# DeltaNet: the blocks M for the row-by-row inverse come by four transfers of 32 partitions instead of one of 128, and are first touched one step later

## The chip, the cores and the metric

One core of a Trainium2 chip. The metric is the device time of one execution in microseconds (us); lower is better.

## What is computed

One decoder layer of 1024 tokens with d_model 1024: a combined projection, dilated attention (A), gated DeltaNet (B), a mix of both, a hierarchical mixture of experts and a per-layer embedding. The change lies in B. It has 8 heads of width 128 and works in chunks of 64 tokens; each chunk needs the inverse of a unit lower triangular matrix:

```python
a_mat = jnp.where(tril_strict, jnp.einsum('nbhid,nbhjd->nbhij', kbeta, kc) * decay_mat, 0.0)
eye = jnp.eye(CHUNK, dtype=jnp.float32)
t_mat = lax.linalg.triangular_solve(eye + a_mat, jnp.broadcast_to(eye, a_mat.shape),
                                    left_side=True, lower=True, unit_diagonal=True)
u = jnp.einsum('nbhij,nbhjd->nbhid', t_mat, vc * bc[..., None])
w = jnp.einsum('nbhij,nbhjd->nbhid', t_mat, kbeta * jnp.exp(gcum)[..., None])
...
def step(state, xs):
    qd, ui, wi, ai, gl, kt = xs
    v_new = ui - jnp.einsum('bhcd,bhde->bhce', wi, state)
    o = jnp.einsum('bhcd,bhde->bhce', qd, state) + jnp.einsum('bhij,bhje->bhie', ai, v_new)
    state = state * jnp.exp(gl)[..., None, None] + jnp.einsum('bhcd,bhce->bhde', kt, v_new)
    return state, o
```

## The kernel before

The layer is one program. In its DeltaNet stage (about 650 to 1290 us of the span) two things run interleaved. The first is the projection: `channels` is a generator that multiplies the normed tokens with the weights of one job (128 output channels) after the other, in two halves of 512 tokens; each half sums 24 matmuls of 128x512 (L37 to L39, three for each product, since both factors are split into a high and a low part) into the PSUM tile mm, of which there are two buffers. Every `next` of it issues six of these matmuls. The last one of a half calls `done`: for q, k and v that is `conv` (L627 to L638, on ScalarE and VectorE), for z it is `job_z` (L669 on ScalarE, then L671 on VectorE; L671 is what sets the PSUM buffer free). Weight tiles wraw come by SP's DMA queue, are split on ScalarE (whi, L182) and VectorE (wlo, L183).

The second is the head's own work. `delta_net` counts steps, 32 for each head; the table P says at which of a head's steps which function issues its instructions: decay at 4 and 5, kk (which fills nat, the blocks of a_mat) at 10 and 13, `solve` at 15, `turned` at 37, `after` at 43. A function with `yield` goes on at the next step. After a step's functions the projection gets its six matmuls. The Python order is only the start: a scheduler in the compiler of the program then fixes the order of the instructions on each engine, and each engine runs its own in that order.

`solve` inverts the 32x32 blocks on the diagonal, 8 token tiles x 4 blocks in one head. L751 writes them from nat to a DRAM tile dA of 32 rows of 1024 numbers, one row for each block. L753 reads that back as M: each of the 4 groups of 32 partitions gets all of dA, 512 KB in all, and each group then computes 8 of the 32 columns of every block's inverse (tu). After three yields L757 sets M's diagonal to one, and 31 row steps follow on VectorE, a multiplication (L764) and a sum (L766) each, whose size grows from row to row, with a yield after every fourth. Then L770 writes tu to DRAM (dT), L774 reads it back as um, `turned` transposes blocks of um (L781), and `after` extends the inverse to 64x64 and runs the scan over chunks: PE multiplies the state S with k (pks, L911), VectorE makes vb of it (L913), PE multiplies vb with um (pvn, L917), ScalarE copies it (vn, L920), PE makes the state's increment (pds, L930) and VectorE the next S (L933 for the first chunk, L936 for the others). So the scan of one head and `solve` of the next share VectorE.

M has one buffer, as most tiles of pool dn. D, the decays, is also filled by a broadcast of 512 KB, in `rows` (L711): one row of 1024 numbers to 128 partitions. L802 multiplies D with PE's products of q and k (pkq, L800); L806 prepares the norms of q (sq); L700 those of k (sk), which the head's later work starts from; L681 transposes k, q and v on PE.

Of the kernel before, what the change touches and what calls it, by code (L numbers as in the profile page):

```python
# [610 lines left out]
class Head:  # L611
# [131 lines left out]
    def solve(self):  # L743


        k, nc, dn = self.k, self.k.nc, self.k.dn
        dA = k.dram.tile([32, 1024], F32, name="dA", bufs=2)
        dT = k.dram.tile([32, 1024], F32, name="dT", bufs=2)
        for b in range(4):
            s = slice(32 * b, 32 * b + 32)  # L750
            nc.sync.dma_start(dA.rearrange("(c b) (r i) -> b r c i", b=4, i=32)[b], self.nat[s, :, s])  # L751
        M = dn.tile([128, 32, 32], F32, name="M")
        nc.sync.dma_start(M.rearrange("p a b -> p (a b)"), dA[None, :, :].to_broadcast([4, 32, 1024]))  # L753
        yield
        yield
        yield
        nc.vector.memset(M.rearrange("p a b -> p (a b)")[:, 0::33], 1.0)  # L757
        tu = dn.tile([128, 8, 32], F32, name="tu")
        nc.vector.tensor_copy(tu, k.id32)
        pr = dn.tile([128, 8, 32], F32, name="prod")  # L760
        for r in range(1, 32):
            n = r + 1
            j = r // 4 + 1
            nc.vector.tensor_tensor(pr[:, :j, :n], tu[:, :j, :n], M[:, None, :n, r].to_broadcast([128, j, n]),  # L764
                                    op=ALU.mult)
            nc.vector.tensor_reduce(tu[:, :j, r], pr[:, :j, :n], axis=AX.X, op=ALU.add)  # L766
            if r % 4 == 0:
                yield
        for g in range(4):
            nc.sync.dma_start(dT.rearrange("q (j g i) -> g q j i", j=8, g=4)[g], tu[32 * g:32 * g + 32])  # L770
        um = k.um[self.h % 2]
        for b in range(4):
            s = slice(32 * b, 32 * b + 32)
            nc.sync.dma_start(um[s, :, s], dT.rearrange("(c b) (m i) -> b m c i", b=4, i=32)[b])  # L774
        yield
# [1163 lines left out]
```

## Time and profile before

| | |
|---|---|
| median of 3 runs | 2029.69 us (2027.57 to 2035.99) |
| the profiled execution | 2035.52 us, span 2033.5 us |
| mean granted clock of TensorE in it | 0.988 |
| PE (matmuls) busy | 1952.7 us, 96% |
| VectorE (DVE) busy | 1162.7 us, 57% |
| ScalarE (ACT) busy | 959.1 us, 47% |
| GpSimd (POOL) busy | 199.4 us, 10% |

The busy shares are means over the whole span. The engines run side by side, and an instruction waits until what it reads has been written; the views further down show for single stretches which engine waited, for what and how long. The times of the rows count from the start of the span.

### The profile page before, as it was taken

The numbers are of one execution on the slowest core, as the hardware profiler recorded it, in microseconds if no ns is written. First come the engines' busy times: TensorE is split into PE (matmuls) and PEld (weight loads), VectorE is DVE, ScalarE is ACT, GpSimd is POOL, SyncE is SP. The second block draws the span as 40 slices with busy tenths as digits, with TensorE's granted clock in tenths as the row PEclk, the third lists the DMA queues.
The fourth block names the chain that finished last, engine by engine and source line by source line (L and its number), as shares of the span: only waits on it lengthen the run. The fifth ranks groups of instructions, "written<-read, shape, count | busy, mean of one in ns | idle before, by whom it ended". The sixth has DMA issues, their size and how long they took to land. (4 is left out here: it accounts for less than half of the span.)

```text
span 2033.5 us, 34133 instructions
## 1 busy us (share of the span) xinstructions
PE 1952.7 (96%) x12954; PEld 1625.6 (80%) x12954; DVE 1162.7 (57%) x2920; ACT 959.1 (47%) x2551; POOL 199.4 (10%) x224
## 2 busy tenths in 40 slices
PE   7999999999999989999999999989999989999898
PEld 7999999989987867777777787877888866666686
DVE  6244434473422587777768874265465466666655
ACT  6344435443533644564565463222433355565643
POOL 0000000000000000001011000120020153321100
PEclk9999999999999999999999999999999989999999
DMA  4112231253133322222232223395366377777642
GB/s 153 56 35 59 74 102 36 81 147 90 53 109 96 81 60 66 79 72 59 73 86 63 72 70 104 118 290 174 125 215 207 118 227 264 246 267 245 243 150 100
DMA packets 247205, 252.48 MB, mean 124 GB/s; under 512 B 63381, under 2 KB 203974, under 8 KB 246778
## 3 DMA queue, kind: packets, MB, share of 16 engines
q1 hardware_dynamic: 229160, 214.40, 34.0%
q0 software_dynamic: 14752, 34.66, 5.0%
q8 instruction: 104, 1.70, 0.4%
q10 hardware_dynamic: 3122, 1.16, 0.2%
q14 instruction: 67, 0.55, 0.1%
HBM read 202.34 MB, written 64.59 MB: 131 GB/s over the span
## 5 line engine op out<-in xcount | busy, mean ns | idle before, releaser
L183 DVE TENSOR_TENSOR wlo<-wraw,whi 128x1024 fp32r<-128x1024 f32 x228 | 275.9, 1223 | 190.4 <-ACT whi L182 188.5
L37 PE MATMUL mm<-whi,hTh 128*128 128x256 f32 x1152 | 336.1, 292 | 6.3 <-ACT sqa L406 3.5
L37 PE MATMUL mm<-hTh,whi 128*128 128x512 f32 x768 | 326.1, 425 | 4.7 <-DVE acc L671 4.7
L38 PE MATMUL mm<-wlo,hTh 128*128 128x256 f32 x1152 | 328.0, 285 | 0.0
L182 ACT ACTIVATE whi<-wraw 128x1024 fp32r<-128x1024 f32 x228 | 237.4, 1057 | 191.9 <-PE mm L38 119.2
L39 PE MATMUL mm<-whi,hTl 128*128 128x256 f32 x1152 | 327.8, 285 | 0.0
L39 PE MATMUL mm<-hTh,wlo 128*128 128x512 f32 x768 | 304.6, 397 | 0.0
L38 PE MATMUL mm<-hTl,whi 128*128 128x512 f32 x768 | 303.4, 395 | 0.0
L37 PEld LDWEIGHTS mm<-whi,hTh 128*128 128x128 f32 x1152 | 221.9, 193 | 18.3 <-issue 7.3
L38 PEld LDWEIGHTS mm<-wlo,hTh 128*128 128x128 f32 x1152 | 222.2, 193 | 0.8 <-DVE wlo L183 0.7
L39 PEld LDWEIGHTS mm<-whi,hTl 128*128 128x128 f32 x1152 | 222.0, 193 | 0.2 <-DVE rsqx L119 0.2
L39 PEld LDWEIGHTS mm<-hTh,wlo 128*128 128x128 f32 x768 | 145.0, 189 | 32.6
L37 PEld LDWEIGHTS mm<-hTh,whi 128*128 128x128 f32 x768 | 146.1, 190 | 30.3 <-DVE acc L671 5.3
L38 PEld LDWEIGHTS mm<-hTl,whi 128*128 128x128 f32 x768 | 146.1, 190 | 22.4
L454 ACT ACTIVATE sm<-sm,nm 128x128 f32<-128x128 f32 (+1 forms) x192 | 84.2, 440 | 87.5 <-DVE nm L452 87.2
L403 ACT ACTIVATE qraw<-mm 128x256 f32<-128x256 f32 x128 | 48.4, 378 | 147.3 <-PE mm L39 147.1
L407 DVE TENSOR_REDUCE ss<-sqa 128x4 f32<-128x256 f32 x96 | 40.1, 418 | 132.1 <-ACT sqa L406 132.0
L636 DVE SCALAR_TENSOR_TENSOR acc<-xp,cols,acc 128x512 f32<-128x512 f32 x144 | 107.7, 748 | 8.1 <-ACT acc L634 5.1
L466 DVE COPY pT<-pt 128x256 f32<-128x256 f32 (+1 forms) x96 | 49.4, 540 | 105.0 <-PE pt L465 105.0
L764 DVE TENSOR_TENSOR prod<-tu,M 128x2 f32<-128x2 f32 (+30 forms) x248 | 83.7, 337 | 6.1
L37 PE MATMUL mm<-whi,mh 128*128 128x256 f32 x256 | 73.8, 290 | 0.8 <-DVE x L1147 0.8
L38 PE MATMUL mm<-wlo,mh 128*128 128x256 f32 x256 | 72.0, 283 | 0.0
(408 smaller groups left out, 3906.3 us busy)
## 6 DMA issues: line engine op xcount, KB each, us to landing
wraw<-in_w_in_dram SPq DMA_DIRECT2D x84, 512.0 KB
wraw<-in_w_expert_down_dram SPq DMA_DIRECT2D x32, 512.0 KB
wraw<-in_w_expert_gate_dram SPq DMA_DIRECT2D x60, 256.0 KB
wraw<-in_w_expert_up_dram SPq DMA_DIRECT2D x60, 256.0 KB
gT<-th SPq DMA_DIRECT2D x32, 256.0 KB
wraw<-in_w_branch_b_dram SPq DMA_DIRECT2D x16, 512.0 KB
gate<-gT SPq DMA_DIRECT2D x32, 256.0 KB
wraw<-in_w_out_dram SPq DMA_DIRECT2D x16, 512.0 KB
```

Source lines behind the costliest of these rows:

```text
L37: nc.tensor.matmul(out, lh, rh, start=start, stop=False)
L38: nc.tensor.matmul(out, lh, rl, start=False, stop=False)
L39: nc.tensor.matmul(out, ll, rh, start=False, stop=stop)
L182: nc.scalar.activation(hi, raw, AF.Copy)
L183: nc.vector.tensor_tensor(lo, raw, r32(hi), op=ALU.subtract)
L403: nc.scalar.activation(rows[t], p, AF.Copy)
L407: nc.vector.tensor_reduce(ss[:, t, :], sq, axis=AX.X, op=ALU.add)
L454: nc.scalar.activation(x.sm[:, h, :nk], x.sm[:, h, :nk], AF.Exp, bias=nm[:, h:h + 1], accum_out=ml[:, x.t, h, 1:2])
L466: nc.vector.tensor_copy(x.pT[:, 2 * pr:2 * pr + 2, :nk], pt[:, :, :nk])
L636: nc.vector.scalar_tensor_tensor(acc, xp[:, i:i + 512], k.conv(i, b), acc, op0=ALU.mult, op1=ALU.add)
L764: nc.vector.tensor_tensor(pr[:, :j, :n], tu[:, :j, :n], M[:, None, :n, r].to_broadcast([128, j, n]), op=ALU.mult)
```

## The change

The single transfer of M, whose source has a leading dimension of 4 with step 0, becomes four transfers of 32 partitions and 128 KB each, all from dA; and the steps between the issue and the first use of M become four instead of three. The rest of `solve` is then one step later too, as its rows are issued by the same generator.

```diff
         M = dn.tile([128, 32, 32], F32, name="M")
-        nc.sync.dma_start(M.rearrange("p a b -> p (a b)"), dA[None, :, :].to_broadcast([4, 32, 1024]))
-        yield
-        yield
-        yield
+        for g in range(4):
+            nc.sync.dma_start(M[32 * g:32 * g + 32].rearrange("p a b -> p (a b)"), dA)
+        for _ in range(4):
+            yield
         nc.vector.memset(M.rearrange("p a b -> p (a b)")[:, 0::33], 1.0)
```

What moves on the engines is seen in their order. On VectorE, where the first head's solve begins (L757 is the memset on M, L764 and L766 the row steps, L638 the end of the convolution of v, L671 the end of z), before the change:

```order
L636 SCALAR_TENSOR_TENSOR acc<-xp,cols,acc 128x512 x3
L757 MEMSET M 128x32
L764 TENSOR_TENSOR prod<-tu,M 128x2
L766 TENSOR_REDUCE tu<-prod 128x1
L764 TENSOR_TENSOR prod<-tu,M 128x3
L766 TENSOR_REDUCE tu<-prod 128x1
L638 SCALAR_TENSOR_TENSOR v_8060<-th,acc 128x512
L764 TENSOR_TENSOR prod<-tu,M 128x4
L766 TENSOR_REDUCE tu<-prod 128x1
L764 TENSOR_TENSOR prod<-tu,M 128x2x5
L766 TENSOR_REDUCE tu<-prod 128x2
L671 SCALAR_TENSOR_TENSOR acc<-th,mm 128x512
```

and with the change, from the same place on:

```order
L636 SCALAR_TENSOR_TENSOR acc<-xp,cols,acc 128x512 x3
L638 SCALAR_TENSOR_TENSOR v_8063<-th,acc 128x512
L671 SCALAR_TENSOR_TENSOR acc<-th,mm 128x512
L806 TENSOR_SCALAR sq<-sq 128x8
L757 MEMSET M 128x32
L764 TENSOR_TENSOR prod<-tu,M 128x2
L766 TENSOR_REDUCE tu<-prod 128x1
L764 TENSOR_TENSOR prod<-tu,M 128x3
L766 TENSOR_REDUCE tu<-prod 128x1
```

L638, L671 and L806 have moved from behind the memset to ahead of it. The second L671 of this job stands 43 rows behind the memset's position before, and 28 rows behind it now; the next L802 stood 27 rows behind the memset and now stands 8 behind it; L700 stands 82 rows behind the memset before and 81 now.

On VectorE in a later head (here the fifth; the third to the eighth have the same rows about the memset but for one or two places of S), before:

```order
L933 COPY S<-pds 128x128
L671 SCALAR_TENSOR_TENSOR acc<-th,mm 128x512
L757 MEMSET M 128x32
L764 TENSOR_TENSOR prod<-tu,M 128x2
L766 TENSOR_REDUCE tu<-prod 128x1
L764 TENSOR_TENSOR prod<-tu,M 128x3
L766 TENSOR_REDUCE tu<-prod 128x1
L806 TENSOR_SCALAR sq<-sq 128x8
L764 TENSOR_TENSOR prod<-tu,M 128x4
L766 TENSOR_REDUCE tu<-prod 128x1
L913 SCALAR_TENSOR_TENSOR vb<-pks,co,vb 128x128
```

and with the change:

```order
L933 COPY S<-pds 128x128
L671 SCALAR_TENSOR_TENSOR acc<-th,mm 128x512
L806 TENSOR_SCALAR sq<-sq 128x8
L913 SCALAR_TENSOR_TENSOR vb<-pks,co,vb 128x128
L802 TENSOR_TENSOR D<-pkq,D 128x512
L757 MEMSET M 128x32
L764 TENSOR_TENSOR prod<-tu,M 128x2
L766 TENSOR_REDUCE tu<-prod 128x1
L764 TENSOR_TENSOR prod<-tu,M 128x3
L766 TENSOR_REDUCE tu<-prod 128x1
L764 TENSOR_TENSOR prod<-tu,M 128x4
```

L806, the first L913 and an L802 now stand ahead of the memset. On SP four rows L754 stand where L753 stood; ahead of the first head's solve and behind the DeltaNet stage the order of no engine differs.

## Rows read from the trace of the kernel before

**Rows 1.** PE's waits, 640 to 1290 us: total, times, longest, in us

```profile
PE pvn L917 <- DVE vb L913: 7.6, 13, 1.5
...
PE mm L37 <- DVE acc L671: 4.7, 2, 4.1
...
PE pk L681 <- DVE k L638: 2.0, 2, 1.8
```

**Rows 2.** What DVE waited for, the same stretch:

```profile
DVE M L757 <- DMA M<-dA: 21.7, 8, 6.7
```

**Rows 3.** DVE's timeline (start, us, instruction, [idle before, releaser]):

```profile
702.49 2.32 DVE L636 SCALAR_TENSOR_TENSOR acc<-xp,cols,acc 128x512 f32<-128x512 f32 x3
711.47 0.09 DVE L757 MEMSET M<- 128x32 f32 x1 [6.66 <-DMA M<-dA]
...
723.39 0.68 DVE L671 SCALAR_TENSOR_TENSOR acc<-th,mm 128x512 f32<-128x512 f32 x1
...
743.17 0.17 DVE L700 TENSOR_SCALAR sk<-sk 128x8 f32<-128x8 f32 x1
...
774.11 0.09 DVE L757 MEMSET M<- 128x32 f32 x1 [4.91 <-DMA M<-dA]
...
849.25 0.09 DVE L757 MEMSET M<- 128x32 f32 x1 [1.36 <-DMA M<-dA]
...
1240.42 0.43 DVE L781 STREAM_TRANSPOSE tm<-um 32x256 f32<-32x256 f32 x1 [1.19 <-DMA um<-dT]
```

**Rows 4.** PE's timeline, the same columns:

```profile
708.96 1.05 PE L800 MATMUL pkq<-q,k 128*128 128x128 f32 x8
...
724.12 0.80 PE L37 MATMUL mm<-hTh,whi 128*128 128x512 f32 x1 [4.12 <-DVE acc L671]
...
728.55 0.63 PE L38 MATMUL mm<-hTl,whi 128*128 128x512 f32 x1
728.98 0.63 PE L39 MATMUL mm<-hTh,wlo 128*128 128x512 f32 x1
...
774.62 0.39 PE L38 MATMUL mm<-hTl,whi 128*128 128x512 f32 x1
774.85 0.40 PE L39 MATMUL mm<-hTh,wlo 128*128 128x512 f32 x1
...
777.56 0.80 PE L911 MATMUL pks<-S,k 128*128 128x128 f32 x2 [2.31 <-DVE S L933]
...
850.82 0.49 PE L917 MATMUL pvn<-vb,um 128*128 128x128 f32 x2 [0.45 <-DVE vb L913]
...
851.37 1.06 PE L800 MATMUL pkq<-q,k 128*128 128x128 f32 x8
...
1209.50 0.49 PE L917 MATMUL pvn<-vb,um 128*128 128x128 f32 x2 [0.48 <-DVE vb L913]
```

**Rows 5.** Three windows (columns in the first line):

```profile
core 0: us, PE busy (x) PEld busy (x) DVE busy (x) ACT busy (x) POOL busy (x), PEclk, DMA share, GB/s
720.00:730.00 10.00, 5.88 (x15) 4.63 (x16) 9.38 (x26) 1.17 (x2) 0.00 (x0) 0.66 0.36 103
775.00:783.00 8.00, 5.69 (x29) 4.78 (x28) 7.21 (x34) 0.65 (x4) 1.64 (x1) 0.79 0.09 35
849.00:922.00 73.00, 70.76 (x456) 56.02 (x455) 56.18 (x149) 40.88 (x134) 6.19 (x4) 1.00 0.26 73
```

**Rows 6.** SP's timeline, the issuing of transfers:

```profile
700.59 0.63 SPq L753 DMA_DIRECT2D M<-dA  x1
...
891.98 0.34 SPq L711 DMA_DIRECT2D D<-Gr  x1
...
1231.51 2.53 SPq L770 DMA_DIRECT2D dT<-tu  x4
```

**Rows 7.** DMA queue, 843 to 849 us (packets, MB, share of 16 engines):

```profile
q1 hardware_dynamic: 187, 0.60, 26.0%
```

**Rows 8.** ACT's timeline, the first use of D:

```profile
896.10 1.16 ACT L719 ACTIVATE eg<-D 128x512 f32<-128x512 f32 x2 [0.99 <-DMA D<-Gr]
```

## The prediction

> **What bounds the kernel now.** The page of the profile comes first: the matmul engine PE is busy 1952.7 of 2033.5 us (96%), the vector engine DVE 57%. A transfer or a DVE row is therefore worth only what PE idles because of it. The change touches the DeltaNet stage alone, about 650 to 1290 us of the span, so the second view is what PE waits for there [rows 1]: the largest groups are all released by DVE; three of them, of 7.6, 4.7 and 2.0 us, stand here. The third is what DVE itself waits for [rows 2]: the tile M at L757, eight times (once for each head), 21.7 us in total and 6.7 at the longest. The reader is to see that these are linked. M's wait is longest in the first two heads, at 711.47 (6.66 us) and 774.11 (4.91 us) [rows 3], and PE's longest waits stand right behind: 4.12 us at 724.12 for the L671 that empties a PSUM buffer, and 2.31 us at 777.56 for a state S [rows 4]. Behind each the granted clock is low for a while: 0.66 in the window 720 to 730, 0.79 in 775 to 783, against 1.00 in 849 to 922 [rows 5]; of the two levels that is a mix of 1.2 and 2.4 GHz. In heads 2 to 7 M is waited for 1.7 us each ((21.7 - 6.66 - 4.91)/6, the first at 849.25), and PE then waits for a vb (first 850.82, last 1209.50, six in all, 5.0 us) [rows 3, 4].
>
> **Why M is late.** In head 0 M is issued at 700.59 [rows 6] and lands when the memset starts, 711.47: 10.9 us for 512 KB. While it moves, the queue fills 26% of the 16 engines' time, with 0.60 MB in 6 us [rows 7]. Another broadcast of 512 KB, D<-Gr, differs in that its 128 partitions are the outermost dimension: issued at 891.98 [rows 6], used at 896.10 [rows 8], 4.1 us. The four transfers after the change have 32 partitions outermost and no repeated dimension, so they are nearer to D's form than to M's.
>
> **The new price of M.** Four issues cost SP what L770's four do, 2.53 us [rows 6], or 0.63 each: 1.9 us more than one. If the bytes then move as D's, M lands at 700.59 + 1.9 + 4.1 = 706.6 in head 0. Bounds: 704.7, where the issues hide wholly in the 4.1 us, and 713.4, where the transfer takes its old 10.9 us and the issues come on top. I take 706.6, since D is the nearest row. The 1.9 us also delay what SP issues next, weight tiles (wraw); I cost that at nothing, because PE's list of waits has no row that ends in a weight tile, and at up to 1.9 us if that cover were gone.
>
> The Trainium skill speaks on both sides, in "DMA: Bandwidth & Descriptors", section "Rules for kernel authors". One row there ("Use all 16 engines") says that a leading repeated dimension of 4 confines a transfer to 4 engines; the 26% agree with that. Another ("Two transfers to disjoint partition halves") says not to bother with splitting, because the parts share the same engines and serialize; by it alone M would land no sooner than before, and only the new order would be left to gain from (rival D). No run so far shows a split M.
>
> **Head 0, step by step.** Removed on PE: the wait of 4.12 us and the slow clock: 12 matmuls 0.43 us apart (728.55 to 728.98) where 0.23 is the pace at full clock (774.62 to 774.85) [rows 4], 12 x 0.20 = 2.4 us. Together 6.5 us. What comes instead is read off the order and the durations. DVE's queue ended its L636 at 702.49 + 2.32 = 704.81 [rows 3]. Behind it now stand L638, L671 and L806 (some 0.7, 0.7 and 0.2 us, and L806 waits for ScalarE's sums of q's squares), so that L757 is reached at about 707.9, and M is there. The second L671 stood 43 rows behind L757 and took 723.39 - 711.47 = 11.9 us to come; now 28 rows lie between, 28/43 x 11.9 = 7.8 us, at 715.7. PE began to wait for it at 724.12 - 4.12 = 720.0. That wait is gone, and the clock has no idle time to fall for.
>
> But DVE has now to keep pace. L757 is 711.47 - 707.9 = 3.6 us earlier, and L638, L671 and L806 (1.6 us) have left the stretch behind it. L802, now 8 rows behind L757, is reached at about 709.4 and waits for pkq until 708.96 + 1.05 = 710.0 [rows 4], 0.6 us. So the far end of the stretch, L700 at 743.17 [rows 3], comes 3.6 + 1.6 - 0.6 = 4.6 us earlier, and not 6.5: the other 1.9 us PE waits for DVE, about what it waits for k (L638) today, 2.0 us [rows 1]. Head 0 gives **4.6 us**. Bounds: 3.0, where L757 is reached 1.6 us later for L806; 8.5, where PE's 2.0 us for k go too.
>
> **Head 1.** Removed: 2.31 us and the clock behind it. The window of 8 us at 0.79 [rows 5] is short of full speed by 8 x 0.21 = 1.7 us, of which some 1.4 fall on busy PE: 3.7 us. M now lands ahead of its memset, since its transfer too is shorter. I set 0.4 us against it for a vb that waits behind other rows: **3.3 us**, 1.4 (a new wait of 2.3 at full clock) to 5.2 (the smaller waits around it go too).
>
> **Heads 2 to 7.** The six waits for vb, 5.0 us in all, have M's wait right ahead of them and vanish: in the order after, vb (L913) stands ahead of L757 and no longer eight rows behind it. But L757 now stands behind L802, which waits for PE's pkq: 851.37 + 1.06 [rows 4], so the row steps begin at about 852.7 and not at 849.25, 3.4 us later, whenever M came. That moves the dense DVE rows on to other S and vb. PE idles 73 - 70.76 = 2.24 us in a head [rows 5], 0.8 of it the vb wait; I put the new waits at 0.3 us for each head, 2 us in all: **+3 us**. Bounds: +5, nothing new waits; -3, each of the six gets a wait of 1.3 us instead.
>
> **The sum.** 4.6 + 3.3 + 3.0 = 10.9 us, from 1.4 to 18.7 us by the bounds. The profiled execution took 2035.52 us, 2 us more than its span and 5.8 more than the median of 2029.69 (runs from 2027.57 to 2035.99); taking the same 10.9 us from each gives 2024.6 beside the one and **2018.8** beside the other. About 0.5% (10 us) is what a measurement of this kernel can tell from no change.
>
> **The rivals.**
> A. The DVE wait only moves. L757 reached 3.4 us later in six heads eats what heads 2 to 7 would give, and in head 0 PE gets the 3.0. For it: DVE is 94% busy in 720 to 730 [rows 5]. Gain 3.0 + 1.4 = 4.4 us, less or more by 3: 2025.
> B. Slower. The row steps end later, so um, which is 8.9 us on its way (dT issued at 1231.51, um waited for until 1240.42 [rows 3, 6]), is late for L781; the S and vb rows queued behind L781 on DVE wait with it, and PE for them. In head 7 L781 already waits 1.19 us. With 3.4 us more, and the clock falling as behind the 2.31 us at 777.56, each of six heads could lose 3 to 4 us of PE: 2029.7 - 7.9 + 18 = 2040. It decides once more than 7.9/6 = 1.3 us for each head is lost. Against it: L781 has its own step, eleven behind that of the last row step.
> C. All waits that stand in M's shadow close, at the upper bounds: 8.5 + 5.2 + 5.0 = 18.7, less 1 for smaller waits that come up: 2012. For it: each of these waits follows one for M. Against it: DVE, 9.38 of 10 us busy in 720 to 730, has little slack to let k come earlier than computed.
> D. Split transfers are no faster. M then lands at 711.5 to 713.4 in head 0; L757 is reached at 707.9 and waits some 4 us. Only the order gives: L638 and the first L671 run ahead of the wait, and the second L671 comes at 713 + 7.8 = 721, about 1 us late and not 4. Of the 10.9 us some 6.5 remain: 2023. Against it: D<-Gr's 4.1 us. It is here that the skill's row on halves would decide.
>
> **How the numbers follow.** Forecast (gain 7 to 15, 2015 to 2023) 0.48; C 0.22; A 0.15; D 0.08; B 0.07. The time predicted is 2019. The range 2009 to 2030 leaves out most of B and the far end of C. Faster by over 0.5% (below 2019.5): 0.6 of the forecast's 0.48 and all of C, 0.51. Within 0.5%: the rest of the forecast, A and D, 0.42. Slower: B, 0.07.
>
> **What would show it.** Right: M's landing within 6 to 7 us of its first issue, the queue's share well over 26% while it moves; no M in DVE's list of waits in heads 0 and 1; PE without the 4.12 and 2.31 us, clock 1.00 in both windows; L757 in head 2 right behind an L802. Wrong: M still in DVE's list with over 4 us at a time (D); PE waits for k, S or vb that add up to as much as before (A); L781 waiting for um in several heads (B); or PE's loss at full clock outside these places, which no step here covers.

## The result, and the profile after

The changed kernel takes 2006.95 us (median of 6 runs, 2002.44 to 2011.04) against 2030.38 us for the kernel before (6 runs, 2027.12 to 2037.12): a ratio of 0.9885, 95% interval 0.9871 to 0.9899. That is 23.4 us, more than twice the 10.9 forecast, and 2 us below the range. The profiled execution took 2005.89 us, span 2003.9, mean clock 0.992.

What PE waited for between 640 and 1290 us in the changed kernel (total, times, longest; the five largest groups; it answers to [rows 1]):

```profile
PE pks L911 <- DVE S L936: 4.6, 12, 0.5
PE pvn L917 <- DVE vb L913: 4.2, 9, 0.8
PE pk L681 <- DVE k L638: 3.9, 7, 2.0
PE mm L37 <- ACT acc L634: 1.3, 2, 0.6
PE px L845 <- DVE tm L781: 0.9, 1, 0.9
```

The waits for L671 and for the first S are gone, and the list of DVE's waits holds no row for M any more ([rows 2] had 21.7 us). DVE's timeline in the first head, and at the memset of the third (it answers to [rows 3]):

```profile
707.22 0.09 DVE L757 MEMSET M<- 128x32 f32 x1
...
715.28 0.68 DVE L671 SCALAR_TENSOR_TENSOR acc<-th,mm 128x512 f32<-128x512 f32 x1
...
732.62 0.69 DVE L638 SCALAR_TENSOR_TENSOR k<-th,acc 128x512 f32<-128x512 f32 x1
...
737.35 0.18 DVE L700 TENSOR_SCALAR sk<-sk 128x8 f32<-128x8 f32 x1
...
842.48 0.69 DVE L802 TENSOR_TENSOR D<-pkq,D 128x512 f32<-128x512 f32 x1 [2.38 <-PE pkq L800]
843.15 0.09 DVE L757 MEMSET M<- 128x32 f32 x1
```

PE's wait for k in the first head, on PE's timeline:

```profile
733.36 0.66 PE L681 MATMUL pk<-ident,k 128*128 128x128 f32 x4 [2.03 <-DVE k L638]
```

Two windows of the changed kernel: heads 0 and 1, and heads 2 to 7 with the end of the stage (columns as in [rows 5]):

```profile
711.00:775.50 64.50, 60.08 (x386) 47.75 (x385) 49.96 (x130) 31.47 (x94) 3.27 (x2) 1.00 0.22 61
839.09:1309.77 470.68, 459.83 (x2952) 374.50 (x2950) 323.07 (x862) 239.53 (x779) 43.23 (x41) 1.00 0.30 87
```

The clock stays at its upper level through heads 0 and 1. The same work as in the second window, from one L39 of the projection to the same L39, took 484.05 us in the kernel before and 472.33 us in e3, a run described below whose PE has the order of before. First the kernel before, then e3:

```profile
848.36:1332.41 484.05, 469.18 (x2952) 375.63 (x2950) 329.39 (x862) 241.50 (x779) 45.10 (x41) 1.00 0.29 84
```

```profile
839.06:1311.39 472.33, 465.44 (x2952) 376.48 (x2950) 328.83 (x859) 241.11 (x779) 45.10 (x41) 1.00 0.30 87
```

The reader is to see that in the changed kernel PE's idle time fell only from 14.87 to 10.85 us, but its busy time by 9.35 us, with the same 2952 matmuls. In e3 it is the other way round: the idle time fell to 6.89 us, and the busy time by 3.74. So waiting can be hidden in the busy time; how much of the 9.35 us is hidden waiting, and how much comes of the changed kernel's other order, is not shown. One place where hidden waiting can be seen is the transposes of the scan's result, before and then after:

```profile
877.78 1.10 PE L899 MATMUL pot<-ident,on 128*128 128x128 f32 x4 [0.25 <-ACT on L894]
```

```profile
866.59 0.60 PE L899 MATMUL pot<-ident,on 128*128 128x128 f32 x4
```

Four transposes that each wait for their own piece (on) show as one row of 1.10 us, of which 0.50 is waiting.

Since the projection's matmuls come in the same sequence in both, the same L39 (mm<-hTh,wlo) is a landmark. Some records of matmuls are missing from each trace, so the landmarks are matched by the instructions around them and not by counting; between the second and the fourth every trace of the table then holds 2952 matmuls. In the kernel before the four stand at 676.27, 848.36, 1204.04 and 1332.41 us. Times from the first to each of the others, in one profiled execution of each kernel (us, and in brackets what is gained on before):

| kernel | M's waits on DVE | first to second (heads 0, 1) | first to third | first to fourth (end of the stage) |
|---|---|---|---|---|
| before | 21.7 | 172.09 | 527.77 | 656.14 |
| changed | 0 | 163.50 (8.6) | 507.91 (19.9) | 634.18 (22.0) |
| fast M, old order (e3) | 0.4 | 162.16 (9.9) | 507.66 (20.1) | 634.49 (21.7) |
| slow M, new order (e4) | 1.7 | 164.30 (7.8) | 508.97 (18.8) | 635.25 (20.9) |
| slower M, new order (e5) | 23.4 | 170.98 (1.1) | 525.58 (2.2) | 653.57 (2.6) |

Nearly all of the gain, 22.0 of the 23.4 us, is made in the DeltaNet stage: 8.6 us in heads 0 and 1, and 13.4 in heads 2 to 7, where 3 were forecast. Behind the stage, where the order is the same, the profiled execution of the kernel before took 6.9 us more than that of the changed one, but it was itself 5 us above its kernel's median; e1 (below) took 1.6 us more there.

### The profile page after: what moved, and what is told of

It reads as the page before. It is cut to its first block, busy times and chain, and to the rows that moved or that the text cites. A ratio compares the mean times of both kernels' runs of the same rounds, so it can differ in the third digit from the quotient of the medians.

```text
span 2003.9 us, 34155 instructions
## 1 busy us (share of the span) xinstructions
PE 1936.3 (97%) x12954; PEld 1619.2 (81%) x12954; DVE 1155.6 (58%) x2920; ACT 957.7 (48%) x2551; POOL 197.0 (10%) x224
## 5 line engine op out<-in xcount | busy, mean ns | idle before, releaser
L39 PE MATMUL mm<-whi,hTl 128*128 128x256 f32 x1152 | 327.7, 284 | 0.0
L39 PE MATMUL mm<-hTh,wlo 128*128 128x512 f32 x768 | 303.0, 395 | 0.0
L39 PEld LDWEIGHTS mm<-whi,hTl 128*128 128x128 f32 x1152 | 221.9, 193 | 0.2 <-DVE rsqx L119 0.2
L39 PEld LDWEIGHTS mm<-hTh,wlo 128*128 128x128 f32 x768 | 144.2, 188 | 31.9
L636 DVE SCALAR_TENSOR_TENSOR acc<-xp,cols,acc 128x512 f32<-128x512 f32 x144 | 107.6, 747 | 6.0 <-ACT acc L634 4.6
L764 DVE TENSOR_TENSOR prod<-tu,M 128x2 f32<-128x2 f32 (+30 forms) x248 | 83.4, 336 | 5.2
```

What stands on the lines that cost most here:

```text
L39: nc.tensor.matmul(out, ll, rh, start=False, stop=stop)
L636: nc.vector.scalar_tensor_tensor(acc, xp[:, i:i + 512], k.conv(i, b), acc, op0=ALU.mult, op1=ALU.add)
```

## The experiments

My theory at this point (S): the faster transfer pays in heads 0 and 1, the new order in heads 2 to 7. Its rivals: the transfer alone (T), the order alone (O), the later step. The first four kernels take the change apart.

**e1, the later step alone.**

```diff
         nc.sync.dma_start(M.rearrange("p a b -> p (a b)"), dA[None, :, :].to_broadcast([4, 32, 1024]))
-        yield
-        yield
-        yield
+        for _ in range(4):
+            yield
```

> The old single transfer, with four yields before the first use. The order of PE's instructions is then that of before, and DVE's nearly so. If the later step is worth something by itself, 2015 to 2025 us; if, as I think, the step alone moves nothing since the scheduler sets the order by its own costs, 2027 to 2033, with M's waits on DVE within 2 us of their 21.7.

Measured: 2030.51 us, ratio 0.999 (0.9975 to 1.0005): no change. M was waited for 24.0 us. The later step is worth nothing.

**e2, the split alone.**

```diff
-        for _ in range(4):
+        for _ in range(3):
             yield
```

> The four transfers with the old three yields. The order on DVE and PE is that of the changed kernel, row for row. If the split (with the order that follows from it) is everything: 2004 to 2010 us, a ratio to before of 0.987 to 0.990. If the later step is part of the gain: 2012 to 2025.

Measured: 2008.6 us, 0.9877 (0.9853 to 0.9901): all of the gain. The new order comes from the split itself, for which the scheduler reckons otherwise than for one transfer, and not from the yields.

**e3, a fast M in the old order.** M's partitions are numbered 4 x block + copy, so that the source has 32 outermost; id32 is set by the partition's remainder by 4 to match.

```diff
-        nc.sync.dma_start(M.rearrange("p a b -> p (a b)"), dA[None, :, :].to_broadcast([4, 32, 1024]))
+        nc.sync.dma_start(M.rearrange("p a b -> p (a b)"), dA[:, None, :].to_broadcast([32, 4, 1024]))
...
-            nc.sync.dma_start(dT.rearrange("q (j g i) -> g q j i", j=8, g=4)[g], tu[32 * g:32 * g + 32])
+            nc.sync.dma_start(dT.rearrange("q (j g i) -> g q j i", j=8, g=4)[g], tu[g::4])
```

> One transfer of 128 partitions whose source has the 32 blocks outermost and the repeat inside (the four copies of a block stand in neighbouring partitions; tu, its start and its way out follow suit), three yields; the order is that of before apart from a few rows of the set-up. Theory S (the transfer gives heads 0 and 1, the order gives much of heads 2 to 7, above all the end of PE's waits for on at L899): M lands 4 to 6 us after its issue, M's waits on DVE fall from 21.7 to under 4 us, PE gains about 9 us in heads 0 and 1 and 3 to 6 us in heads 2 to 7, 2014 to 2019 us. Rival T (only the transfer counts): 2005 to 2009. Rival O (only the order counts): 2027 to 2032.

Measured: 2009.89 us, 0.9889 (0.987 to 0.9907). M's issue on SP and the memset on DVE in the first head:

```profile
702.05 0.54 SPq L756 DMA_DIRECT2D M<-dA  x1
```

```profile
705.91 0.09 DVE L760 MEMSET M<- 128x32 f32 x1 [0.41 <-DMA M<-dA]
```

3.9 us instead of 10.9, from one transfer of the same 512 KB. The old order with a fast M gains as much as the change: S falls, T is not contradicted (the median is 0.9 us above T's range, and the interval reaches into it).

**e4, a slow M in the new order.** dA gets a gap behind each group of 8 blocks, so that its slowest dimension stays 4; the rest of solve uses the same numbering of the blocks.

```diff
-        dA = k.dram.tile([32, 1024], F32, name="dA", bufs=2)
+        dA = k.dram.tile([4, 9, 1024], F32, name="dA", bufs=2)
...
-            nc.sync.dma_start(M[32 * g:32 * g + 32].rearrange("p a b -> p (a b)"), dA)
+            nc.sync.dma_start(M[32 * g:32 * g + 32].rearrange("p a b -> p (a b)"), dA[:, 0:8, :])
```

> Four transfers of 32 partitions as in the change and its order row for row, but dA is laid out as 4 groups of 8 blocks with a gap behind each, so that the slowest dimension of the source is 4 and not 32. Theory S: each transfer uses about a quarter of the 16 engines, M lands 11 to 13 us after the first issue, DVE waits 4 to 7 us for it in heads 0 and 1 and not in heads 2 to 7; the time is 2012 to 2019 us. Rival T: 2027 to 2032, all of the gain is gone. Rival O: 2005 to 2009.

Measured: 2008.91 us, 0.9882 (0.9863 to 0.9901). This too gains it all, and T falls with it. The rows of the first head, on SP and DVE:

```profile
701.17 2.75 SPq L754 DMA_DIRECT2D M<-dA  x4
```

```profile
710.16 0.09 DVE L757 MEMSET M<- 128x32 f32 x1 [1.72 <-DMA M<-dA]
```

M took 9.0 us from the first issue, so it was slow, but the new order reaches the memset later. The issue of M for the third head on SP, before and in the changed kernel:

```profile
839.88 0.56 SPq L753 DMA_DIRECT2D M<-dA  x1
```

```profile
830.73 1.73 SPq L754 DMA_DIRECT2D M<-dA  x4
```

In the changed kernel DVE comes to the memset at 843.15, 12.4 us behind the first issue; before it wanted to at 849.25 - 1.36 = 847.89, 8.0 us behind [rows 3]. Either half of the change takes M's wait off DVE, and once it is off the other half has nothing left to take. This made a new theory (W): what costs is the time that DVE's in-order queue stands still at the memset, however it comes about. Its rival is O.

**e5, an M slow enough to be waited for in the new order.** As e4, with 2 groups of 16 blocks.

```diff
-        dA = k.dram.tile([4, 9, 1024], F32, name="dA", bufs=2)
+        dA = k.dram.tile([2, 17, 1024], F32, name="dA", bufs=2)
...
-            nc.sync.dma_start(M[32 * g:32 * g + 32].rearrange("p a b -> p (a b)"), dA[:, 0:8, :])
+            nc.sync.dma_start(M[32 * g:32 * g + 32].rearrange("p a b -> p (a b)"), dA[:, 0:16, :])
```

> As the slow M in the new order, but dA in 2 groups of 16 blocks with a gap behind each, so that the slowest dimension of each transfer is 2; the order is again that of the changed kernel row for row. If the slowest dimension sets how many engines a transfer uses, M lands some 15 to 20 us after its first issue. The memset of heads 2 to 7 is reached 12.4 us behind the issue in the new order, so DVE waits 3 to 8 us in each head. Theory W (what costs is DVE's in-order queue standing still at the memset, whatever the order; 21.7 us of it cost 23 us): the time is 2008 us plus 1 to 1.3 times the sum of M's waits on DVE, 2035 to 2065 us. Rival O (the order is what gained): 2005 to 2015.

Measured: 2027.43 us, 0.9974 (0.9963 to 0.9985). The waits on DVE were smaller than expected in most heads; the row of the list and the first head:

```profile
DVE M L757 <- DMA M<-dA: 23.4, 8, 7.2
```

```profile
700.03 2.69 SPq L754 DMA_DIRECT2D M<-dA  x4
```

```profile
714.47 0.09 DVE L757 MEMSET M<- 128x32 f32 x1 [7.21 <-DMA M<-dA]
```

PE's waits between 640 and 1290 us show where it lands: the wait for L671 of the kernel before is back, and S is waited for longer than in the changed kernel (4.6):

```profile
PE pks L911 <- DVE S L936: 10.7, 21, 1.7
...
PE mm L37 <- DVE acc L671: 4.0, 1, 4.0
```

With the order of the changed kernel and 23.4 us of waiting nearly all of the gain is lost: 18.5 us by the medians for 21.7 us of waits more than e4. In the old order, e3 against before, it is 21.3 us of waits and 1.1% of the time, some 22 us. The landmarks give 18.3 and 21.7 us. O falls; W stands, with a price of 0.85 to 1.05 us for each us of M's wait. My range for e5 was too high by the size of the waits, and a little by the price of 1 to 1.3 (with 23.4 us it would give 2031 to 2038).

**e6 and e7, small rows first.** To the fast M of e3, the scheduler's priority for ro, and then for the convolution of k.

```diff
-            nc.vector.tensor_tensor(so, so, self.rq[:, c4], op=ALU.mult)
-            nc.vector.tensor_tensor(so, so, self.rq[:, c4], op=ALU.mult)
-            rstd_pow(k, ro, so, 128.0)
-            nc.vector.tensor_tensor(ro, ro, self.rq[:, c4], op=ALU.mult)
+            with hp():
+                nc.vector.tensor_tensor(so, so, self.rq[:, c4], op=ALU.mult)
+                nc.vector.tensor_tensor(so, so, self.rq[:, c4], op=ALU.mult)
+                rstd_pow(k, ro, so, 128.0)
+                nc.vector.tensor_tensor(ro, ro, self.rq[:, c4], op=ALU.mult)
```

```diff
-            for i in range(3):
-                nc.vector.scalar_tensor_tensor(acc, xp[:, i:i + 512], k.conv(i, b), acc, op0=ALU.mult, op1=ALU.add)
...
+            with k.tc.high_priority(offset=P["hp"]) if j == 1 else ExitStack():
+                for i in range(3):
+                    nc.vector.scalar_tensor_tensor(acc, xp[:, i:i + 512], k.conv(i, b), acc, op0=ALU.mult, op1=ALU.add)
```

> The fast single transfer in the old order, and the four small DVE rows that make ro (the two of so, the scale, the last of ro) get the scheduler's higher priority, as vb and S have. If PE's waits for on at L899 in heads 2 to 7 come from these rows standing behind row steps on DVE: the waits are gone, 3 to 5 us less than with the fast transfer alone, 2004 to 2008 us. If ahead of the row steps they only push vb and S back: 2009 to 2014 us.

> As the kernel with ro first, and the convolution of k too gets the higher priority. If PE's wait for k at L681 in heads 0 and 1 (2 to 4 us) is only a matter of the order: 2 to 3 us less again, 2002 to 2006. If the convolution's long DVE rows (0.75 us each) then hold up vb and S: 2007 to 2015.

Measured: 2013.95 us, 0.9907 (0.989 to 0.9924), and 2013.84 us, 0.9906 (0.9888 to 0.9924). Both are misses, some 4 us over e3 (the intervals just overlap). PE's waits of e6 between 640 and 1290 us:

```profile
PE pks L915 <- DVE S L940: 10.6, 18, 1.2
PE pk L684 <- DVE k L641: 3.7, 2, 1.9
PE pvn L921 <- DVE vb L917: 1.7, 4, 0.6
```

No row for pot is left (e3's list has 1.2 us), but S is waited for 10.6 us, where e3's list has 3.9. The waits for on went, and more came back at S: the second outcome of e6. The wait for k did not go in e7 (4.0 us).

**e8 and e9, wlo on GpSimd.** Less work on DVE, if W were about its load: in the changed kernel and in e3.

```diff
-        return wload(k, wcols(k.I["w_in"][0], (jobs[i][0], 128)))
+        return wsplit(k, wraw(k, wcols(k.I["w_in"][0], (jobs[i][0], 128))), k.nc.gpsimd)
...
-    nc.vector.tensor_tensor(lo, raw, r32(hi), op=ALU.subtract)
+    (eng or nc.vector).tensor_tensor(lo, raw, r32(hi), op=ALU.subtract)
```

> The changed kernel, and the low part of the projection's weights (wlo, L183, 1.2 us each, some 4 in a head) is computed on GpSimd instead of VectorE. If it is DVE's queue time in general that sets the pace of the stage, as the price of M's waits suggests, PE's remaining waits for DVE (some 13 us between 640 and 1290 us) shrink by half or more and the time is 1997 to 2003 us. If only the standing still at one place counts, 2004 to 2010. If GpSimd is too slow for it, or its work slows DVE down, PE waits for wlo and the time is over 2010.

> The same with the fast single transfer of M in the old order. The same three outcomes, 2 us above those of the kernel before it: 1998 to 2005, 2006 to 2012, or over 2012 us.

Measured: 2050.37 us, 1.0103 (1.0082 to 1.0124), and 2048.25 us, 1.0084 (1.0067 to 1.0101): slower than the kernel before. PE waits for vb and S, and not for wlo. GpSimd's timeline and DVE's at one place of e8:

```profile
878.55 2.39 POOL L183 TENSOR_TENSOR wlo<-wraw,whi 128x1024 fp32r<-128x1024 f32 x1
```

```profile
878.61 2.35 DVE L891 TENSOR_TENSOR ro<-ro,rq 128x4 f32<-128x4 f32 x1
```

A row of four columns that takes 0.16 us in the other kernels lasts as long as GpSimd's instruction beside it. So these two say nothing on DVE's load; they add standing still in another form (DVE's L636 went from 747 to 911 ns in the mean). The order of PE moved as well, so the 43 us are not put down to this alone.

**e10, work in place of the wait.**

```diff
         nc.vector.memset(M.rearrange("p a b -> p (a b)")[:, 0::33], 1.0)
+        idle = dn.tile([128, 1], F32, name="idle")
+        for _ in range((6, 4, 2, 2, 2, 2, 2, 2)[self.h]):
+            nc.vector.tensor_reduce(idle, M.rearrange("p a b -> p (a b)"), axis=AX.X, op=ALU.add)
```

> The changed kernel, and behind the memset on M the sum over all of M into one column, which nothing uses, as often as fills about what M's wait was: 6 times in head 0, 4 in head 1, twice in the others, 22 rows of some 1.1 us, 24 us in all. The scheduler knows of this work and orders around it, also on PE. Theory W (DVE's time at this place costs PE about its own length, waiting or busy): 2023 to 2035 us. If a wait costs more than work, since an order made for work goes around it: 2010 to 2020 us.

Measured: 2029.41 us, 0.999 (0.9975 to 1.0005). Its rows on DVE, all together:

```profile
L760 DVE TENSOR_REDUCE idle<-M 128x1 f32<-128x1024 f32 x22 | 26.7, 1214 | 0.1
```

26.7 us of work cost 22.5 us. That agrees with W in amount, but not as a proof of it: PE's order is another one, and its list is led by waits for acc (12.8 us) and tm (6.6 us).

**e11, less work on DVE.**

```diff
-            for i in range(3):
+            for i in range(1, 3):
                 nc.vector.scalar_tensor_tensor(acc, xp[:, i:i + 512], k.conv(i, b), acc, op0=ALU.mult, op1=ALU.add)
```

> The changed kernel with two instead of three of the convolution's DVE rows for each half (L636; one tap of the convolution is left out, so 48 rows of 0.75 us, 36 us of DVE, are gone; the order shifts with it). If DVE's time still costs PE one to one after the change: 1972 to 1985 us. If only what PE still waits for between 640 and 1290 us is to be had, some 15 us: 1992 to 2000. If DVE has slack again and PE sets the pace alone: 2003 to 2009.

Measured: 2013.67 us, 0.9911 (0.9883 to 0.9938). In the stage itself, from the first to the fourth landmark, it takes 637.50 us, 3.3 more than the changed kernel: 36 us less of DVE's work gained nothing. It loses another 5.6 us behind the stage, where it works on other numbers; I did not follow that, and the kernel before and the changed one differ by 6.9 us there. So a lighter DVE does not shorten the stage after the change. Of the three outcomes the last is the nearest, though the time is 5 us above its range, and since PE's order moved too, this one run does not prove it.

One more row speaks against a price on all of DVE's idle time. In the changed kernel DVE waits at L802 for PE's pkq, by the list of what DVE waited for between 640 and 1290 us:

```profile
DVE D L802 <- PE pkq L800: 18.1, 9, 2.8
```

In the kernel before, and in e3, it is 2.2 us, once. In each of heads 2 to 7 these are 2.38 us right ahead of the memset, longer than DVE stood there for M before (2.12 us at most); yet the stage takes as long as in e3 (634.18 and 634.49 us). So W must be put more narrowly: not DVE's time as such, nor any stop of its queue, but a stop for a transfer at a place where S and vb stand right behind. At L802 DVE waits for PE's own work, and vb stands ahead of it; which of the two spares the time is not shown.

No version beat the changed kernel beyond its interval; e3 ties with it, with one transfer in place of four.

## Why the prediction was wrong

**Right.** The direction, and head 0 nearly row by row: L757 at 707.22 (707.9 forecast), the second L671 at 715.28 (715.7), no wait for it and no slow clock, the wait for k back at 2.03 us (1.9). The changed execution is 0.68 us ahead already at the first landmark (675.59 against 676.27); L700 came 743.17 - 737.35 = 5.8 us earlier, 5.1 without that (4.6). Heads 0 and 1 together gave 8.6 us where 7.9 were forecast. L757 of head 2 does stand right behind an L802. DVE found M there 7.3 us behind its first issue; the four issues cost SP 1.71 us, not 2.53:

```profile
699.92 1.71 SPq L754 DMA_DIRECT2D M<-dA  x4
```

Of the later um (rival B) one wait of PE for tm shows, 0.9 us, in the list above.

**The step that failed** is the term of heads 2 to 7, +3 with bounds of -3 and +5; it measured 13.4. It priced M's wait by the six waits for vb in PE's list, 5.0 us, on the premise that a row of DVE is worth only what PE is seen to idle for it. DVE stands still for M for 10.1 us in these heads, and PE pays about that and more: e3, whose PE has the same order as before, gains 484.05 - 472.33 = 11.7 us there for 10.1 us of waits taken away. Of these, 8.0 us were idle time of PE, where I had put 5.0 down to M, and 3.7 were counted as busy. One head shows how. PE's timeline before, and the same three instructions in e3:

```profile
993.10 0.39 PE L38 MATMUL mm<-hTl,whi 128*128 128x512 f32 x1
...
994.90 0.49 PE L917 MATMUL pvn<-vb,um 128*128 128x128 f32 x2 [1.17 <-DVE vb L913]
...
1000.45 0.49 PE L911 MATMUL pks<-S,k 128*128 128x128 f32 x2 [0.27 <-DVE S L936]
```

```profile
979.74 0.39 PE L38 MATMUL mm<-hTl,whi 128*128 128x512 f32 x1
...
980.20 0.39 PE L920 MATMUL pvn<-vb,um 128*128 128x128 f32 x2
...
985.20 0.38 PE L914 MATMUL pks<-S,k 128*128 128x128 f32 x2
```

The lead of e3 grows from 13.36 to 14.70 at pvn, to 15.25 at pks, and to 16.39 behind the head's second pot (1048.22 against 1031.83): 3.0 us for an M wait of 2.07. Only 1.17 of it is the row I counted. The rest comes as the queue, once late, stays late for the next S and for on, whose waits stand in other rows of the list (0.27 us at this pks, 0.56 at the second pot), and in pieces counted as busy, such as the second matmul of the pvn pair.

The 2 us set against it for new waits did come, in other rows than I had named: in heads 2 to 7 PE waits 3.1 us for acc (L634), k and vn, which the list of before lacks there. The order does put the row steps later, but PE's waits for S and vb did not grow with it; in these heads they fell from 12.5 to 7.6 us.

**The rivals.** C, all waits in M's shadow, was the nearest by number, but by luck: it gave heads 0 and 1 13.7 us, which measured 8.6, and heads 2 to 7 5.0 us from the same list, which measured 13.4. Of A the condition came, as DVE's wait moved to L802, but not the price; B did not happen beyond the 0.9 us. D was decided by e3 to e5, for the form and not for the number of transfers. The slowest dimension of the source sets the speed: 10.9 us with 4 outermost in one transfer, 9.0 with 4 in each of four, 14.4 with 2 in each of four, 3.9 with 32 in one. The queue's share while M moves goes with it: 26.0% with 4 outermost before [rows 7], and here e4 (4 in each) from 836 to 840 us, e5 (2 in each) from 848 to 852, and the changed kernel (32 in each, with a weight tile in the same stretch) from 700 to 706:

```profile
q1 hardware_dynamic: 112, 0.41, 25.6%
```

```profile
q1 hardware_dynamic: 53, 0.21, 12.8%
```

```profile
q1 hardware_dynamic: 1232, 1.05, 60.2%
```

These are about 4 and 2 of the 16 engines, and more than half of them. The Trainium skill says in "DMA: Bandwidth & Descriptors", section "Rules for kernel authors", under "Use all 16 engines", that the slowest dimension sets how many engines a transfer uses; the shares agree. Its other row there, one 128-partition transfer rather than parts, agrees with e3, which needs no split.

**The change's own parts.** I had costed the transfer and the later step as two things. e1 and e2 show that the step is worth nothing, and e3 and e4 that the split does two things of which either suffices: M lands sooner, and the scheduler puts its first use later.

**What stays open.** A us of M's wait costs 1.2 us in heads 2 to 7 in the old order (before against e3, 11.7 us for 10.1), and 0.8 in the new one (e5 against e4, (653.57 - 170.98) - (635.25 - 164.30) = 11.6 us for 23.4 - 8.5 = 14.9), by one profiled execution of each. What stands behind the memset differs between the two orders; I did not take this apart further.

## What to carry to other kernels

Price an in-order engine's wait for a transfer by its own length first, and take something off only where the trace shows slack for what is queued behind it. A wait for the very engine that bounds the kernel is another case: the 18.1 us at L802 cost nothing that shows. The bounding engine's list of waits shows only part of what a late chain costs, so compare landmarks or windows with their busy times too, and make sure that a landmark is the same instruction in both traces. When two edits each take away the same wait, test them one at a time: here either half gave everything. When a transfer repeats a source, put the long dimension outermost and the repeat inside; numbering the partitions to suit it cost nothing that shows here.

## What the runs showed of the hardware

GpSimd's subtraction of two 128x1024 tiles (2.4 us, against 1.2 on VectorE) held up VectorE rows with two inputs in SBUF until it ended: 2.35 us for a 128x4 row that takes 0.16. The Trainium skill has this in "SBUF — State Buffer", section "Who interferes with whom": the port pair that the two share is locked for a whole instruction, and a VectorE row with two SBUF inputs contends for it with a GpSimd instruction that reads SBUF. The run agrees.

In the window of heads 0 and 1 the granted clock stayed at 1.00 after the changed kernel's wait of 2.03 us at 733.36, while it was 0.79 in 775 to 783 before, with the wait of 2.31 us at 777.56.
